# A four-layer hybrid model: two first mixers set later among the filling tiles, sums into x and evacuations of q and k put ahead on their engines

## The chip, the cores and the metric

The kernel runs on one core of one Trainium2 chip. The metric is the device time of one execution in microseconds. The core's engines work in parallel, each through its own queue: TensorE (PE; its weight loads are listed as PEld), VectorE (DVE), ScalarE (ACT), GpSimd (POOL) and SyncE (SP), which here only issues transfers.

## What is computed

1040 tokens (16 meta tokens and 1024 of the sequence) with 1024 features go through four layers, each a normalisation, a projection in, a mixer and a projection out that is added to x:

```python
for i in range(DEPTH):                       # 4
    kind, j = i % N_MIXERS, i // N_MIXERS    # 3 kinds
    u = rmsnorm(h, norm_gain[i])
    if kind == 0:
        y = attention_branch(u, ...)   # 16 heads of q, 4 of k and v, window 128, rope, sinks
    elif kind == 1:
        y = mlstm_branch(u, ...)       # 8 heads, causal conv on q and k, blocks of 128
    else:
        y = hgrn2_branch(u, ...)       # 8 heads, decay per feature
    h = h + jnp.where(valid[None, :, None], y, 0.0)
```

In the second kind (`mlstm`) q and k pass a convolution over four tokens and a SiLU; two gates per head give rows of cumulated decays; then, block by block, a product of k and q weighted by these rows, and a state C carried from block to block. In the third kind (`hgrn2`) the product of q and k is formed level by level with decays in between. In the first kind q and k are normalised per head and rotated (rope) before windowed attention.

## The kernel before, in words

x lies in SBUF for the whole run, features on partitions, in eight tiles `x[:, m, :]`. All work on tokens goes in three chunks of 400, 384 and 256 columns (`CHUNKS`), or in nine blocks (`blk`: one of 16 tokens, eight of 128). To keep fp32 accuracy every factor of a large product is split into a high and a low part (`split`, L193 on ScalarE and L194 on VectorE: `uh`, `ul` from the normalised x, `wh`, `wl` from the weights, `yh`, `yl` from a mixer's result), and three matmuls are made for each product.

**The order on TensorE is written by hand.** The program is a list of steps `[cost, function, pre]`; the cost is in ns of matmul columns at 2.4 per ns (`MM`). `weave(a, b)` merges two lists in proportion to their costs; `later`, `spread` and `chain` put steps at a given distance. A step `[c, lambda: None, None]` does nothing and only takes up c in these sums. At the end the list is run through once. A step's `pre` (load a matrix of weights in two halves into `wr` on SyncE's queue, L205, and split it) is written out as soon as the costs of the steps up to it come to less than `LOOKAHEAD` = 12000.

**The order on the other engines** is not the written one: among the instructions whose inputs and buffers are free, the program's scheduler prefers the one that was written first. Inside `with tc.high_priority(offset=PRIO)` (`PRIO` = 40) an instruction ranks as if written 40 instructions earlier. Steps of the mixers and the splits of `yh`, `yl` are wrapped in it already (`hi`).

Buffers: eight PSUM banks for everything (`psum`, tags pj for projections, pm, po, pt, pa for the mixers and the statistics), six temporaries (`TMPS`), three pairs of split weights, two raw halves (`RAWS`).

**Where the change lies:**

- `proj_out` (L290 to L333): for each chunk and each of eight output tiles m, six matmuls (L321) and then the sum into x on VectorE (L324), which frees the bank. At a layer's last products `fin` follows, which squares the new x for the next norm (L351) and adds the squares up (L355).
- `qk_proj` of `layer_a`: `evac` copies a finished chunk of q or k out of PSUM twice on ScalarE, scaled (L491) and squared (L492), and issues four transfers that rotate the partitions (L495). 2000 later in the list, TensorE sums the squares over the head (L506), from which ScalarE makes the reciprocal root (L337, L338); VectorE applies rope (L511 to L514). In the mixer of this layer, a score step (matmuls L597 and L598, minimum L604, exponential L607, reciprocal L609, product on GpSimd L610) is followed two steps later by a transpose on TensorE (L622).
- `layer_b`, the second layer: `head` is v of head 0 with the gates, `body` begins with q and k of head 0 (`conv_proj`: copy L825, four steps of convolution L828 and L831, SiLU L399 to L403, product L835 or L837). `gate_rows` (L776 to L794) makes the decay rows on eight partitions and writes them to DRAM. Then for each head h its mixer is woven with q, k and v of head h + 1. A mixer begins with a step of no cost that reads two decay rows back, spread over all partitions (`rb` L856, `wb` L857); each block has steps `s1` (product of k and q, L864, transpose of k, L866), `s2` (L885, L887), `s3` (L899, state C at L904) and `s4` (L913).
- `layer_c`, the third layer: for each head, `main` holds five regions of eight levels (X, made at L1111 to L1114 on VectorE and ScalarE) with their matmuls (`levels_mm`: L1127, L1137), `tails` what follows. `weave(main[r], last)` joins each region with the tail of the one before, and the whole is woven with `fill`: what is left of q of head 0, and f and q of head 1.

Of the kernel before, what the change touches and what calls it, by code (L numbers as in the profile page):

```python
# [11 lines left out]
AF = mybir.ActivationFunctionType  # L12
ALU = mybir.AluOpType
# [23 lines left out]
PRIO = 40  # L37
ROWS, TMPS, RAWS, YS = 8, 6, 2, 3
XS = 14
GAP, BURST = 200.0, 1300.0  # L40
GATE_LAG, GATE_COLS = 2000.0, 17000.0
KT_LAG, ATT_LAG = 900.0, 600.0
NORM_AT = (4000.0, 0.7), (5000.0, 0.5), (8000.0, 0.5)
Y_LAST, Y_EARLY, Y_AHEAD = 3, 8, 2500.0
# [66 lines left out]
def hybrid_kernel(ctx: ExitStack, tc: tile.TileContext, ins, out, layers=(0, 1, 2, 3)):  # L111
    nc = tc.nc
    v, s, g, pe, sp = nc.vector, nc.scalar, nc.gpsimd, nc.tensor, nc.sync
# [11 lines left out]
    def nm(x):  # L125
        ctr[0] += 1
        return f"{x}{ctr[0]}"
# [19 lines left out]
    def psj():  # L147
        return psum("pj", 3)
# [15 lines left out]
    x = cpool.tile([P, KT, T], F32, name="x")  # L164
# [27 lines left out]
    def split(src, h, l):  # L192
        s.copy(h, src)  # L193
        v.tensor_tensor(l, src, h.bitcast(F32), op=ALU.subtract)  # L194
# [90 lines left out]
    def hi(fn):  # L285
        def f():
            with tc.high_priority(offset=PRIO):
                fn()

        return f  # L290

    def proj_out(src0, src1, y, chunks=CHUNKS, fin=None, inrow=False):
        st = {}

        def pre0():
            st[0] = weights(src0, "o", inrow=inrow)

        def pre1():
            st[1] = weights(src1, "o", inrow=inrow)

        groups = []
        for n, (c0, cn) in enumerate(chunks):
            grp = []

            def ysplit(k, n=n, c0=c0, cn=cn):
                def fn():
                    yh, yl = (tpool.tile([P, 400], F32R, tag=z, name=nm(z), bufs=YS)[:, :cn] for z in ("yh", "yl"))
                    split(y(k)[:, c0 : c0 + cn], yh, yl)
                    st["y", n, k] = yh, yl

                return [0.0, hi(fn), None]

            def product(m, k, n=n, c0=c0, cn=cn):
                h, l = st[m // 4]
                mc = slice((m % 4) * P, (m % 4 + 1) * P)
                if k == 0:
                    st["p", n, m] = psj()
                acc = st["p", n, m]
                yh, yl = st["y", n, k]
                for i, (a, b) in enumerate(((h, yh), (h, yl), (l, yh))):  # L320
                    pe.matmul(acc[:, :cn], a[:, k, mc], b,  # L321
                              start=(k == 0 and i == 0), stop=(k == 1 and i == 2))
                if k == 1:
                    v.tensor_tensor(x[:, m, c0 : c0 + cn], x[:, m, c0 : c0 + cn], acc[:, :cn], op=ALU.add)  # L324
                    if fin:
                        fin(m, n, c0, cn)

            order = [(m, k) for m in range(KT - Y_LAST) for k in range(2)]
            order += [(m, k) for k in range(2) for m in range(KT - Y_LAST, KT)]
            for m, k in order:  # L330
                pre = (pre0, pre1)[m // 4] if (n == 0 and m % 4 == 0 and k == 0) else None
                grp.append([3 * cn * MM, lambda m=m, k=k, product=product: product(m, k), pre])
            groups.append(([ysplit(0), ysplit(1)], grp))  # L333
        return groups
# [80 lines left out]
    def layer_a(i, j, first, last, fin):  # L415
        win, wout = ins["a_win"][j], ins["a_wout"][j]
        chunks = LAST_CHUNKS if last else CHUNKS
        R = {}
# [66 lines left out]
        def qk_proj(src, gcol, work, fsplit, ch):  # L485
            late = {}

            def evac(acc, n, c0, cn):
                dst, sq, rot = work(n, c0, cn)
                late[n] = dst, sq, rot  # L490
                s.activation(dst, acc[:, :cn], AF.Identity, scale=R["cons"][:, gcol : gcol + 1])  # L491
                s.activation(sq, acc[:, :cn], AF.Square)  # L492
                for q in range(4):
                    o = q ^ 1
                    sp.dma_start(rot[32 * q : 32 * q + 32], dst[32 * o : 32 * o + 32])  # L495

            def finish(n, c0, cn):
                def stat():
                    dst, sq, rot = late[n]
                    b0, bn = CHUNKS[n]  # L500
                    if R.get("cs", (None,))[0] != n:
                        R["cs"] = n, R["mix"].tile([P, 2, 400], F32, tag="cs", name=nm("cs"), bufs=1)
                        sp.dma_start(R["cs"][1][:, :, :bn], ins["rope"][:, :, b0 : b0 + bn].rearrange("a p t -> p a t"))
                    late[n] = dst, sq, rot, R["cs"][1][:, :, c0 - b0 : c0 - b0 + cn]
                    st = psa()
                    pe.matmul(st[:, :cn], R["masks"][:, 0:P], sq, start=True, stop=True)  # L506
                    rstd_from(st, sq, cn, 64)

                def rope():
                    dst, sq, rot, cos_sin = late[n]  # L510
                    v.tensor_tensor(dst, dst, cos_sin[:, 0, :cn], op=ALU.mult)  # L511
                    v.tensor_tensor(rot, rot, cos_sin[:, 1, :cn], op=ALU.mult)
                    v.tensor_tensor(dst, dst, rot, op=ALU.add)
                    v.tensor_tensor(dst, dst, sq, op=ALU.mult)  # L514

                return [(D_Q[0], [4 * cn * MM, stat, None]), (D_Q[1], [0.0, rope, None]),
                        (D_Q[2], fsplit(lambda: late[n][0], n, c0, cn))]

            return proj(src, evac, ch), [finish(n, *c) for n, c in enumerate(ch)]
# [212 lines left out]
    def layer_b(i, j, fin):  # L732
        win, wout = ins["b_win"][j], ins["b_wout"][j]
        R = {}
# [257 lines left out]
        for h in range(8):  # L992
            mx = mixer(h)
            mx, rest = mx[:-3], mx[-3:]
            if h < 7:
                body += weave(mx, flat(qg[h + 1]) + flat(kg[h + 1]) + flat(vg[h + 1]))
                if h < 6:
                    body += weave(rest, gates(h)[:6]) + gates(h)[6:] + flat(zg[h][1]) + flat(outs(oc[h]))
                else:
                    held = rest  # L1000
            else:
                body += weave(held + mx, gates(6) + flat(zg[6][1]))
# [3 lines left out]
    def layer_c(i, j, fin):  # L1006
        win, wout = ins["c_win"][j], ins["c_wout"][j]
        R = {}
# [261 lines left out]
        for h in range(8):  # L1270
            fill = qg[0][2] if h == 0 else []
            if h in (4, 6):
                fill += flat(outs(oc[h - 3]))
            if h < 7:
                fill += flat(fg[h + 1]) + flat(qg[h + 1])
            if h in (1, 3, 5):
                fill += flat(vg[h // 2 + 1])
            for z in {2: (0, 1), 4: (2,), 5: (3,), 7: (4, 5, 6)}.get(h, ()):
                fill += flat(zg[z])
            main, tails, end = mixer(h)  # L1280
            if h:
                tails[0].append(held)
            held = end
            mx = []
            for r in range(5):
                mx += weave(main[r], last)
                last = [[TAIL_LAG, lambda: None, None]] + tails[r]
            body += weave(mx, fill)
# [190 lines left out]
```

## Time and profile before

| | before |
|---|---|
| median of 3 runs | 2635.76 us (2635.3 to 2638.44) |
| the profiled execution | 2632.63 us, its span 2630.8 us |
| granted TensorE clock, mean | 0.995 |
| DVE, ACT, POOL busy | 75%, 64%, 9% of the span |

The first layer runs up to about 490 us of the span, the second to about 1576, the third to about 2178, the fourth to the end. In lines of the timeline, the first number is the start in us, the second the length in us, and what stands in brackets is the idle time of the engine just before and what ended it. "L506 <- ACT t L492" in a list of waits reads: line 506 waited for the instruction of line 492 on ScalarE that writes a tile t. In a table of stretches the busy times of the engines come in the order PE, PEld, DVE, ACT, POOL, each with its count of instructions, and then the granted clock (1.00 is full).

### The profile page before, as it was taken

What the parts mean: (1) busy time and instruction counts of PE and PEld (TensorE: products, weight loads), DVE (VectorE), ACT (ScalarE), POOL (GpSimd) and SP (SyncE); (2) the same over time, 40 slices, a digit from 0 to 9 for tenths busy, and PEclk for the clock granted to TensorE, in tenths of its full rate; (3) what the DMA queues carried; (4) which work ended last, traced back from release to release, by engine and by line L of the source; (5) the groups of instructions that cost most, each with busy time, mean ns of one, the idle gap of its engine ahead of it and who ended that gap; (6) DMA issues with size and microseconds to landing.
All of it is one profiled execution on the core that took longest, in us unless ns stands there. A gap on an engine that the chain in (4) does not pass through costs nothing.

```text
span 2630.8 us, 53986 instructions
## 1 busy us (share of the span) xinstructions
PE 2562.9 (97%) x20246; PEld 2468.6 (94%) x20246; DVE 1976.8 (75%) x5344; ACT 1693.7 (64%) x4374; POOL 249.5 (9%) x502
## 2 busy tenths in 40 slices
PE   7999999989999999999999999999999999999999
PEld 5899989989999999999999999999999998999999
DVE  7887798784747474757475688988888989887896
ACT  7777767565454545454545757878675857867772
POOL 2221231000000000000000000101000000321330
PEclk9999999999999999999999999999999999999999
DMA  4213111011111111111111101111110113212112
GB/s 129 69 49 91 47 44 48 22 63 52 41 57 41 57 41 57 41 53 45 53 45 49 53 30 42 34 34 34 38 38 30 38 50 92 63 39 83 55 37 80
DMA packets 82581, 135.89 MB, mean 52 GB/s; under 512 B 12032, under 2 KB 35712, under 8 KB 82320
## 3 DMA queue, kind: packets, MB, share of 16 engines
q1 hardware_dynamic: 82320, 132.45, 15.9%
q8 instruction: 159, 2.61, 0.4%
q14 instruction: 102, 0.84, 0.1%
HBM read 117.56 MB, written 4.26 MB: 46 GB/s over the span
## 4 chain that ended last, share of the span: by engine, by line
PE 74%; DVE 12%; ACT 8%; DMA 3%; issue 2%; SPq 1%; POOL 1%; DVEq 0%; ACTq 0%; POOLq 0%
PE pj L227 35%; PE pj L321 15%; PE pj L276 10%; ACT Sm L607 1%; PE po L641 1%; PE po L885 1%; PE pt L622 1%; PE pa L899 1%; PE po L887 1%; DVE Sm L604 1%; DVE wl L194 1%; DMA cs<-in_rope 1%; PE pj L272 1%; DVE Pl L625 1%; PE pm L1137 1%
## 5 line engine op out<-in xcount | busy, mean ns | idle before, releaser
L227 PE MATMUL pj<-uh,wh 128*128 128x256 f32 (+2 forms) x2688 | 919.7, 342 | 9.4 <-ACT uh L193 9.4
L227 PE MATMUL pj<-ul,wh 128*128 128x256 f32 (+2 forms) x2688 | 867.2, 323 | 2.7 <-DVE ul L194 2.4
L227 PE MATMUL pj<-uh,wl 128*128 128x256 f32 (+2 forms) x2688 | 863.8, 321 | 0.0
L227 PEld LDWEIGHTS pj<-uh,wh 128*128 128x128 f32 x2688 | 509.3, 189 | 28.6 <-ACT uh L193 13.1
L227 PEld LDWEIGHTS pj<-ul,wh 128*128 128x128 f32 x2688 | 509.5, 190 | 13.8 <-DVE ul L194 6.4
L227 PEld LDWEIGHTS pj<-uh,wl 128*128 128x128 f32 x2688 | 509.0, 189 | 0.1
L193 ACT CAST wh<-wr 128x512 fp32r<-128x512 f32 (+1 forms) x338 | 202.9, 613 | 102.0 <-PE pj L321 31.3
L194 DVE TENSOR_TENSOR wl<-wr,wh 128x512 fp32r<-128x512 f32 (+1 forms) x338 | 232.1, 697 | 48.5 <-ACT wh L193 45.0
L321 PE MATMUL pj<-yh,wh 128*128 128x384 f32 (+2 forms) x768 | 253.1, 330 | 9.9 <-DVE x L324 6.4
L324 DVE TENSOR_TENSOR x<-x,pj 128x384 f32<-128x384 f32 (+2 forms) x480 | 234.6, 509 | 34.1 <-PE pj L321 32.7
L321 PE MATMUL pj<-yl,wh 128*128 128x384 f32 (+2 forms) x768 | 245.3, 319 | 0.3 <-DVE yl L194 0.3
L321 PE MATMUL pj<-yh,wl 128*128 128x384 f32 (+2 forms) x768 | 245.2, 319 | 0.0
L276 PE MATMUL pj<-wh,uh 128*128 128x256 f32 (+1 forms) x768 | 231.9, 302 | 0.0
L276 PE MATMUL pj<-wl,uh 128*128 128x256 f32 (+1 forms) x768 | 216.5, 282 | 0.0
L276 PE MATMUL pj<-wh,ul 128*128 128x256 f32 (+1 forms) x768 | 216.2, 281 | 0.0
L607 ACT ACTIVATE Sm<-Sm,s 128x257 f32<-128x257 f32 (+2 forms) x272 | 130.7, 482 | 91.7 <-DVE s L604 90.3
L610 POOL TENSOR_TENSOR Sm<-Sm,s 128x512 f32<-128x512 f32 (+2 forms) x136 | 141.2, 1038 | 467.1 <-DVE s L609 454.3
L403 ACT ACTIVATE t<-t 128x384 f32<-128x384 f32 (+2 forms) x240 | 117.8, 491 | 88.0 <-DVE t L402 86.4
L402 DVE SCALAR_TENSOR_TENSOR t<-pj,t 128x384 f32<-128x384 f32 (+2 forms) x192 | 98.8, 515 | 81.7 <-ACT t L401 80.0
L321 PEld LDWEIGHTS pj<-yh,wh 128*128 128x128 f32 x768 | 144.2, 188 | 14.7 <-DVE x L324 8.6
L193 ACT CAST yh<-r 128x384 fp32r<-128x384 f32 (+2 forms) x120 | 57.1, 478 | 146.2 <-PE pj L321 132.5
L276 PEld LDWEIGHTS pj<-wh,uh 128*128 128x128 f32 x768 | 144.6, 188 | 2.1
(251 smaller groups left out, 5445.7 us busy)
## 6 DMA issues: line engine op xcount, KB each, us to landing
wr<-in_b_win SPq DMA_DIRECT2D x124, 256.0 KB, 2.8
wr<-in_a_win SPq DMA_DIRECT2D x80, 256.0 KB, 2.9
wr<-in_c_win SPq DMA_DIRECT2D x64, 256.0 KB, 2.8
wr<-in_a_wout SPq DMA_DIRECT2D x32, 256.0 KB, 2.8
wr<-in_b_wout SPq DMA_DIRECT2D x32, 256.0 KB, 2.7
t<-t SPq DMA_DIRECT2D x104, 48.0 KB, 2.0
cs<-in_rope SPq DMA_DIRECT2D x11, 400.0 KB, 3.7
cs<-in_rope SPq DMA_DIRECT2D x11, 384.0 KB, 3.2
```

The costliest lines, as they stand in the source:

```text
L193: s.copy(h, src)
L194: v.tensor_tensor(l, src, h.bitcast(F32), op=ALU.subtract)
L227: pe.matmul(acc[:, :cn], a[:, k, :], b[:, k, c0 : c0 + cn], start=(k == 0 and i == 0), stop=(k == KT - 1 and i == 2))
L272: pe.matmul(acc[:48, :nc], um[0][:, k, :], m[:, kk, :], start=(k == 0 and m is wh), stop=(k == KT - 1 and m is wl))
L276: pe.matmul(acc[:cn, :nc], a[:, k, c0 : c0 + cn], m[:, kk, :], start=(k == 0 and j == 0), stop=(k == KT - 1 and j == 2))
L321: pe.matmul(acc[:, :cn], a[:, k, mc], b, start=(k == 0 and i == 0), stop=(k == 1 and i == 2))
L324: v.tensor_tensor(x[:, m, c0 : c0 + cn], x[:, m, c0 : c0 + cn], acc[:, :cn], op=ALU.add)
L402: v.scalar_tensor_tensor(a[:, :cn], z, 0.0, a[:, :cn], op0=ALU.min, op1=ALU.subtract)
L403: s.activation(a[:, :cn], a[:, :cn], AF.Exp)
L604: v.tensor_tensor_reduce(Sm[:nq, u, :nk], S[:nq, u, :nk], R["masks"][:nq, P + mo : P + mo + nk], -1.0, sinks[u], ALU.add, ALU.min, st[:nq, ...
L607: s.activation(Sm[:nq, u, : nk + 1], Sm[:nq, u, : nk + 1], AF.Exp, scale=-1.0, bias=st[:nq, u : u + 1], accum_out=den[:nq, u : u + 1])
L610: g.tensor_tensor(Sm[:nq, :, :nk], Sm[:nq, :, :nk], den[:nq].rearrange("p (u c) -> p u c", c=1).to_broadcast([nq, 2, nk]), op=ALU.mult)
```

## The change

Four edits. In the second layer, a step of cost 8000 that does nothing is put ahead of the mixer of head 0, before it is woven with q, k and v of head 1. In the third layer, the same with 2500 ahead of the first region of head 0. The sums into x in `proj_out`, and the two copies out of PSUM in `evac` of q and k, get the rank of an instruction written 40 earlier. No arithmetic, buffer or transfer is added or removed.

```diff
-GATE_LAG, GATE_COLS = 2000.0, 17000.0
+GATE_LAG, GATE_COLS, MIX_AHEAD, START_LAG = 2000.0, 17000.0, 8000.0, 2500.0
...
                 if k == 1:
-                    v.tensor_tensor(x[:, m, c0 : c0 + cn], x[:, m, c0 : c0 + cn], acc[:, :cn], op=ALU.add)
+                    with tc.high_priority(offset=PRIO):
+                        v.tensor_tensor(x[:, m, c0 : c0 + cn], x[:, m, c0 : c0 + cn], acc[:, :cn], op=ALU.add)
                     if fin:
                         fin(m, n, c0, cn)
...
             def evac(acc, n, c0, cn):
                 dst, sq, rot = work(n, c0, cn)
                 late[n] = dst, sq, rot
-                s.activation(dst, acc[:, :cn], AF.Identity, scale=R["cons"][:, gcol : gcol + 1])
-                s.activation(sq, acc[:, :cn], AF.Square)
+                with tc.high_priority(offset=PRIO):
+                    s.activation(dst, acc[:, :cn], AF.Identity, scale=R["cons"][:, gcol : gcol + 1])
+                    s.activation(sq, acc[:, :cn], AF.Square)
                 for q in range(4):
...
         for h in range(8):
             mx = mixer(h)
             mx, rest = mx[:-3], mx[-3:]
+            if h == 0:
+                mx.insert(0, [MIX_AHEAD, lambda: None, None])
             if h < 7:
                 body += weave(mx, flat(qg[h + 1]) + flat(kg[h + 1]) + flat(vg[h + 1]))
...
             held = end
-            mx = []
+            mx = [] if h else [[START_LAG, lambda: None, None]]
             for r in range(5):
                 mx += weave(main[r], last)
```

## The prediction, made before the changed kernel was run

> **What bounds the kernel now.** I read the page's first block, then the waits of PE, then the timeline around each long one.
>
> ```profile
> span 2630.8 us, 53986 instructions
> PE 2562.9 (97%) x20246; PEld 2468.6 (94%) x20246; DVE 1976.8 (75%) x5344; ACT 1693.7 (64%) x4374; POOL 249.5 (9%) x502
> ```
>
> PE sets the end: 2562.9 of 2630.8 us. Whatever this change does can only come out of the 67.9 us in which PE does nothing, or out of a slow clock behind such a pause, because it removes no matmul.
>
> ```profile
> PE pa L506 <- ACT t L492: 9.3, 7, 2.2
> PE pm L864 <- DVE r L837: 8.9, 1, 8.9
> PE pt L622 <- POOL Sm L610: 6.5, 7, 2.1
> PE pj L321 <- DVE x L324: 6.4, 6, 1.4
> ...
> PE pm L1137 <- DVE X L1114: 2.1, 1, 2.1
> PE pm L597 <- DVE x L324: 1.8, 1, 1.8
> ```
>
> Columns: total us, times, longest. Of the pauses, four kinds touch the edited lines: L864 is the first mixer matmul of the second layer, L1137 lies in the first mixer of the third, L324 is the sum into x, L492 the second evacuation of q or k. Together 8.9 + 2.1 + 6.4 + 1.8 + 9.3 = 28.5 us. L622 belongs to the attention chain, which the edit touches only through the order on ACT and DVE.
>
> What a pause costs afterwards is seen in the granted clock (columns: stretch, length, busy us of PE, PEld, DVE, ACT, POOL, clock, DMA share, GB/s):
>
> ```profile
> 545.80:554.70 8.90, 0.01 (x1) 0.02 (x2) 8.55 (x23) 6.07 (x15) 0.00 (x0) 0.67 0.25 91
> 554.70:559.10 4.40, 4.40 (x17) 4.33 (x18) 3.44 (x10) 2.94 (x8) 0.00 (x0) 0.50 0.18 60
> 559.10:565.00 5.90, 5.90 (x30) 4.62 (x29) 3.43 (x12) 2.66 (x8) 0.10 (x1) 1.00 0.01 3
> ...
> 1651.00:1654.80 3.80, 3.80 (x43) 3.74 (x36) 3.55 (x14) 2.50 (x9) 0.00 (x0) 0.55 0.02 4
> ...
> 2385.40:2388.80 3.40, 3.38 (x10) 3.18 (x11) 3.27 (x7) 3.26 (x9) 1.14 (x1) 0.52 0.25 87
> ```
>
> After the 8.9 us pause PE works 4.40 us at half clock: 2.2 us lost. After the pause of L1137, 3.80 us at 0.55 lose 1.7; after the longest pause of L506, 3.40 us at 0.52 lose 1.6. So the ceiling is 28.5 + 5.5 = 34.0 us.
>
> **The second layer's lead (8000 ns ahead of the mixer of head 0).** PE's order is written by hand, so the lead moves PE's instructions for certain.
>
> ```profile
> 545.49 0.28 PE L227 MATMUL pj<-uh,wl 128*128 128x256 f32 x1
> 554.68 0.23 PE L864 MATMUL pm<-q,r 128*16 128x16 f32 x2 [8.92 <-DVE r L837]
> ```
>
> ```profile
> 531.64 2.31 DVE L780 TENSOR_TENSOR_SCAN r<-r,r 8x1040 f32<-8x1040 f32 x1
> 533.88 2.68 DVE L783 TENSOR_TENSOR_SCAN r<-ones,r 8x16 f32<-8x16 f32 x9
> 554.07 0.57 DVE L837 SCALAR_TENSOR_TENSOR r<-r,t 128x400 f32<-128x400 f32 x1
> ```
>
> PE has finished q and k of head 0 at 545.8 and waits for the first columns of k, whose convolution ends on DVE at 554.6: DVE was late with it after the gate rows (two of whose steps are shown, 5.0 us). By the code's own costs the mixer of head 0 (without its last three steps) is 14,650 and its filling tiles 42,987. With the lead, 8000 of 22,650 = 35.3% of the filling goes first: 15,183, so 17 steps of 960 to 1000 (640 for the short chunk): all of q of head 1 and five steps of its k, 15.4 us. The mixer's first matmul then comes no sooner than 545.8 + 15.4 = 561.2, and its k is ready at 554.6: 6.6 us to spare. Saved: 8.9 + 2.2 = 11.1.
>
> What is late next? Those 17 steps hand DVE more convolutions while it is still behind.
>
> ```profile
> 560.00:600.00 40.00, 40.00 (x268) 38.40 (x268) 29.57 (x89) 23.53 (x63) 0.49 (x5) 1.00 0.10 31
> ```
>
> ```profile
> 600.00:610.00 10.00, 10.00 (x82) 9.81 (x81) 2.05 (x9) 2.83 (x8) 0.10 (x1) 1.00 0.10 38
> ```
>
> From 545.8 to 600 DVE does 8.55 + 3.44 + 29.57, about 42 us (0.9 us lie between the rows); PE will be there 11.1 us sooner, after 43.1 us. DVE would have to be 98% busy, if its work stayed where it is. It doesn't: the lead moves four fifths of the mixer's DVE work behind k of head 1, where now, at 600 to 610, DVE is busy 2.05 of 10 us. The waiting convolutions keep their PSUM banks meanwhile.
>
> ```profile
> 546.68 0.47 ACT L825 COPY t<-pj 128x400 f32<-128x400 f32 x1
> ...
> 556.29 0.34 ACT L825 COPY t<-pj 128x256 f32<-128x256 f32 x1
> ```
>
> The three chunks of k of head 0 were all done on PE at 545.8 and left PSUM from 546.7 to 556.6: three of eight banks are tied up by such a backlog, five are left for one running product and the four kinds of mixer banks. I take 1.0 us for what this adds: 10.1 saved. Bounds: 11.1 if nothing new appears, 0 if the whole pause moves to another wait.
>
> Moved with the mixer are its two broadcast reads on SP (rb, wb), and the lead counts as 8000 of the 12,000 by which weights are announced, so q's weights of head 1 are announced some 4 us ahead instead of 12. Both matter only if the queues follow the written order closely.
>
> ```profile
> 520.02 1.29 DVE L194 TENSOR_TENSOR wl<-wr,wh 128x512 fp32r<-128x512 f32 x2 [7.34 <-ACT wh L193]
> 524.20 0.69 DVE L194 TENSOR_TENSOR wl<-wr,wh 128x512 fp32r<-128x512 f32 x1 [2.89 <-ACT wh L193]
> 525.08 0.69 DVE L194 TENSOR_TENSOR wl<-wr,wh 128x512 fp32r<-128x512 f32 x1 [0.18 <-ACT wh L193]
> ...
> 528.67 0.68 DVE L194 TENSOR_TENSOR wl<-wr,wh 128x512 fp32r<-128x512 f32 x1
> ...
> 531.04 0.67 DVE L194 TENSOR_TENSOR wl<-wr,wh 128x512 fp32r<-128x512 f32 x1
> ```
>
> There are three weight buffers: the splits at 520 are q's of head 0, those at 524 and 525 its k's, those at 528.7 and 531.0 q's of head 1, ready 14 us before PE is free for them: more than 12 ahead, so they run when a buffer is free, not when they are announced. I cost this at nothing; if the cover goes, they queue behind DVE's backlog up to 554.6, and 554.6 - 545.8 = 8.8 us of the saving is gone.
>
> [...] The row: a 2.1 us pause before 1651 is followed by clock 0.55. [...]
>
> **The third layer's lead (2500 ns).** By the same arithmetic the first mixer has 27,159 against 23,360 of filling. The pause isn't at its beginning:
>
> ```profile
> 1650.84 0.33 PE L1137 MATMUL pm<-X 128*32 128x32 f32 x16 [2.10 <-DVE X L1114]
> ```
>
> It is its fourth region, some 17,100 into the mixer (1260 + 2900 + 2900 of the regions before it, 2848 + 3595 of the tails woven into those, some 3600 of its own levels and the tail beside them). Ahead of that stand 17,100/27,159 = 62.9% of the filling now, 19,600/29,659 = 66.0% then: 0.7 us more. DVE is busy all through (3.55 of 3.80 us in the row from 1651), so the work, not the start, is late. I take 0.8 saved; bounds 3.8 (pause and clock gone) and minus 2.1 (such a pause once more, from a denser mixer).
>
> **Sums into x ahead (L324).** All 20 output products are touched; the seven pauses total 6.4 + 1.8 = 8.2 us. One of them:
>
> ```profile
> 2175.56 1.29 DVE L194 TENSOR_TENSOR wl<-wr,wh 128x512 fp32r<-128x512 f32 x2 [0.24 <-ACT wh L193]
> 2176.77 0.55 DVE L355 TENSOR_TENSOR t<-t,t 128x384 f32<-128x384 f32 x1
> 2177.24 0.55 DVE L324 TENSOR_TENSOR x<-x,pj 128x384 f32<-128x384 f32 x1
> ```
>
> The sum frees the bank PE waits for. It gets the rank of an instruction written 40 earlier, some six products' matmuls: the norm's squares (L355) fall behind it, weight splits announced 12 us ahead don't. I take two thirds, 5.5. Bounds 8.2 and 0; a loss would be the norm's, and is in the last term.
>
> **Evacuations of q and k ahead (L491, L492).** The seven pauses total 9.3 us, 10.9 with the clock.
>
> ```profile
> 2382.60 0.62 ACT L193 CAST wh<-wr 128x512 fp32r<-128x512 f32 x1
> 2383.12 0.48 ACT L491 ACTIVATE t<-pj,cons 128x256 f32<-128x256 f32 x1
> ...
> 2385.00 0.36 ACT L492 ACTIVATE t<-pj 128x256 f32<-128x256 f32 x1
> ```
>
> ```profile
> 256.08 0.70 PE L506 MATMUL pa<-t,masks 128*128 128x256 f32 x2 [1.82 <-ACT t L492]
> ```
>
> ```profile
> 254.56 0.47 ACT L491 ACTIVATE t<-pj,cons 128x256 f32<-128x256 f32 x1 [1.03 <-DVE t L513]
> 255.64 0.38 ACT L492 ACTIVATE t<-pj 128x256 f32<-128x256 f32 x1 [0.61 <-DVE t L514]
> ```
>
> At 2383 ACT was busy with other work, which a higher rank can pass. At 255 it was idle, waiting for DVE to release a buffer: rank can't help there, and that pause (1.8 us, up to 256.1) stays. Of the other 9.1 I take 5.0; bounds 9.1 and 0. The four DMAs behind each evacuation go out with it, so SP is held less, not more.
>
> **New waits.** What goes ahead puts something back: attention's exponentials, unit splits, squares. Nearest row: L622, 6.5 us in seven pauses. I take half as much again, 3.0; bounds 0 and 31 (the rival below).
>
> **Sum:** 10.1 + 0.8 + 5.5 + 5.0 - 3.0 = 18.4 us, against the profiled execution's own 2632.63 (span 2630.8 and 1.8 around it): 2614.2. The median is 3.1 above that execution: **2617.4**.
>
> **Rivals.** *Leads alone*: the priorities give and take the same; 10.9 us, 2624.9. For it: waits in the attention layers are many and short. Against: rows like 2176.77, where a square stands ahead of the sum.
>
> *The wait moves*: the second layer's pause comes back as a wait for weights or banks, 8.8 of 11.1 lost, and 10.1 becomes 2.3: 2625.2. For it: the 98%. Against: the free DVE from 600. With "leads alone" as well it would be 2632.7, no change; that is also what a change that misses its aims would look like.
>
> *Slower*: the evacuations, at the attention chain's own rank, delay it on ACT.
>
> ```profile
> L491 ACT ACTIVATE t<-pj,cons x54: 452/566/605, 27.3 to 2482.9; 128x384 f32<-128x384 f32 x26, 128x256 f32<-128x256 f32 x18, 128x400 f32<-128x400 f32 x10
> L492 ACT ACTIVATE t<-pj x54: 361/483/509, 27.7 to 2484.0; 128x384 f32<-128x384 f32 x26, 128x256 f32<-128x256 f32 x18, 128x400 f32<-128x400 f32 x10
> ```
>
> A pair takes 0.566 + 0.483 = 1.05 us, and with the six into rows there are 60. If half of them push an exponential back when its transpose has no slack, that is 31 us: 2617.4 + 31 = 2648. It makes the kernel slower by over 0.2% from 23 of 60 on ((18.4 + 5.3) / 1.05). Against: PE waits for that chain only seven times now.
>
> **How the numbers follow.** 0.2% is 5.3 us, about what a measurement of this kernel can tell from no change. Forecast 0.60 (its own range 2606 to 2624), leads alone 0.15, the wait moves 0.08, both or a miss 0.07, slower 0.10. Faster 0.60 + 0.15 + 0.08 = 0.83, same 0.07, slower 0.10. The low end takes every upper bound, 11.1 + 3.8 + 8.2 + 9.1 = 32.2 us: 2603.5, so 2604; the high end is 2630, which leaves out the last two cases, 0.17.
>
> **What would show it.** Right: no wait of L864 for L837, clock 1.00 from 540 to 600 in the second layer; fewer and shorter waits of L321 for L324 and of L506 for L492, that at 256 still there; the third layer's pause near 1640 little changed. Wrong: PE waits for wl or for L825 near 546 to 575 (the wait moved); L622's total well above 6.5 or L363's waits for L355 at the layers' ends (the priorities took as much as they gave).

## The result, and the profile after

| | before | after |
|---|---|---|
| median | 2635.47 us (12 runs) | 2639.16 us (12 runs) |
| ratio, 95% interval | | 1.0014 [1.0005, 1.0023] |
| span of the profiled execution | 2630.8 us | 2633.3 us |

No faster: 2639.16 lies 3.7 us above before and 9 us above the upper end of the predicted range. The page's first block of the changed kernel, then its waits of PE (total us, times, longest):

```profile
span 2633.3 us, 53915 instructions
PE 2564.4 (97%) x20246; PEld 2468.9 (94%) x20246; DVE 1979.8 (75%) x5344; ACT 1692.1 (64%) x4374; POOL 250.6 (10%) x502
```

```profile
PE pa L364 <- DVE t L356: 14.7, 5, 5.0
PE pa L508 <- ACT t L494: 12.4, 9, 3.2
...
PE pt L624 <- POOL Sm L612: 8.7, 16, 1.2
...
PE pm L1141 <- DVE X L1118: 2.1, 3, 0.9
...
PE pj L321 <- DVE x L325: 1.1, 2, 0.7
...
PE po L887 <- DVE W L874: 0.9, 1, 0.9
...
PE pm L599 <- DVE x L325: 0.4, 1, 0.4
```

Lines below the edits are one to four numbers higher than before. The sum into x is now L325, the add of squares L356, the statistics of the norm L364; the evacuations are L493 and L494, the head sum L508.

Two aims are met: the 8.9 us pause of L864 is gone, and the waits for the sum into x fell from 8.2 us (6.4 + 1.8) to 1.5. Two things rose: the statistics' wait for the adds of squares, now 14.7 us in five pauses, and the head sums' wait for the evacuations, from 9.3 to 12.4 us, the very wait that the evacuations' rank was to shorten. Before has that row with two pauses only, at the program's start:

```profile
PE pa L363 <- DVE t L355: 5.5, 2, 4.9
```

The other three are new, one at the end of each of the first three layers. The timeline of PE, after:

```profile
259.08 1.22 PE L508 MATMUL pa<-t,masks 128*128 128x256 f32 x2 [3.19 <-ACT t L494]
...
500.12 0.97 PE L364 MATMUL pa<-t,ones 128*128 128x384 f32 x2 [3.55 <-DVE t L356]
...
1580.30 1.65 PE L364 MATMUL pa<-t,ones 128*128 128x384 f32 x2 [2.92 <-DVE t L356]
...
2185.34 0.91 PE L364 MATMUL pa<-t,ones 128*128 128x384 f32 x2 [2.88 <-DVE t L356]
```

The second layer's beginning in stretches (columns as in the prediction):

```profile
545.20:559.00 13.80, 13.80 (x98) 13.54 (x97) 12.65 (x29) 8.14 (x23) 0.00 (x0) 1.00 0.35 121
559.00:570.00 11.00, 11.00 (x72) 11.00 (x71) 9.81 (x25) 7.30 (x18) 0.00 (x0) 1.00 0.15 49
570.00:580.00 10.00, 9.13 (x56) 7.54 (x55) 9.30 (x24) 6.55 (x18) 0.10 (x1) 1.00 0.17 52
```

PE is busy throughout at full clock, but for one pause of 0.87 us at 575.88. DVE is busy 31.76 of 34.80 us, 91%: the full engine that I feared is there, and it doesn't stop PE.

To place gains and losses I compare when PE begins its n-th matmul in two kernels (worked out from the traces; the number of matmuls is the same). Each row is how late the kernel is against before, in us, at the matmul that before begins at the time on top; minus is ahead:

```
                 260     480     500     545     640    1560    1600    2175    2200    2215    2629
after           4.32    5.65    9.61    9.61   -0.03    1.08    5.47    4.65    6.09    4.90    2.49
leads           0.18    0.62    0.63    0.63   -7.71   -7.60   -7.56   -7.14   -7.14   -7.15   -6.83
leads_ev        5.45    6.48    6.46    6.47   -3.33   -3.15   -3.12   -3.95   -3.95   -3.31    0.05
leads_x         2.46    2.94    6.85    6.85   -1.50   -1.45    1.71    1.62    4.91    3.73    2.82
leads_xmid      2.43    2.93    3.30    3.30   -5.06   -4.86   -4.83   -4.97   -4.95   -4.99   -6.39
leads_x_add     2.29    3.01    5.49    5.49   -4.28   -3.94   -1.26   -0.78    1.36    1.37    1.24
leads_x_sq     -0.35    0.48    5.80    5.80   -4.18   -4.17   -0.04   -0.65    6.21    4.45    4.50
leads_ev_xmid   5.34    6.68    7.02    7.03   -2.66   -1.64   -1.59   -2.42   -2.40   -0.23   -1.57
start_only      1.19    1.30    1.29    1.29    1.26    1.26    1.26    1.12    1.12    1.11    1.41
leads_12        1.20    1.50    1.51    1.51   -8.44   -8.01   -7.98   -7.65   -7.63   -7.71   -6.91
leads_ev_wh     6.52    6.75    6.76    6.77   -3.01   -2.87   -2.83   -3.00   -1.11   -1.02   -0.61
leads_ev_rope   0.22    1.31    1.31    1.31   -8.47   -8.30   -8.26   -8.23   -8.22   -2.40   -3.41
leads_ev_two    0.27    0.96    0.95    0.96   -8.72   -8.62   -8.58   -8.94   -8.66   -8.64   -8.55
```

The first row tells the story of the change: 5.65 us lost in the first layer, 4.0 more at its end, 9.6 won by the second layer's lead (9.61 to -0.03), 4.4 lost at that layer's end, 1.4 at the third's, 3.6 won back in the last layer. The other rows are the experiments.

Each row is one execution, and that sets how finely it can be read. VectorE and ScalarE do the same instructions in the same order in before, start_only, leads and leads_12 through the whole first layer, and yet these four stand up to 1.5 us apart at 480. leads_x and leads_x_sq, in the same order up to 486 us, stand 2.5 us apart there: in leads_x two stretches of half clock came (at 128 us, where the clock is 0.57 over 4.00 us, last section, and at 258 us), about 1.7 us each, and in leads_x_sq none. So a step of one or two us in a single row shows little; steps of 3 us and more that several rows repeat, and the medians of several runs, carry the argument.

### The profile page after: what moved, and what is told of

Read it like the earlier page. It is cut to its first block, busy times and chain, and to the rows that moved or that the text cites. A ratio compares the mean times of both kernels' runs of the same rounds, so it can differ in the third digit from the quotient of the medians.

```text
span 2633.3 us, 53915 instructions
## 1 busy us (share of the span) xinstructions
PE 2564.4 (97%) x20246; PEld 2468.9 (94%) x20246; DVE 1979.8 (75%) x5344; ACT 1692.1 (64%) x4374; POOL 250.6 (10%) x502
## 4 chain that ended last, share of the span: by engine, by line
PE 74%; DVE 12%; ACT 8%; DMA 2%; issue 2%; SPq 1%; POOL 0%; DVEq 0%; ACTq 0%; POOLq 0%
PE pj L227 35%; PE pj L321 14%; PE pj L276 10%; ACT Sm L609 1%; PE po L887 1%; PE po L643 1%; PE pt L624 1%; PE pa L901 1%; DVE Sm L606 1%; DVE wl L194 1%; PE po L889 1%; DVE x L325 1%; PE pj L272 1%; PE pm L1141 1%; DVE qs L464 1%
## 5 line engine op out<-in xcount | busy, mean ns | idle before, releaser
L227 PEld LDWEIGHTS pj<-uh,wh 128*128 128x128 f32 x2688 | 509.1, 189 | 28.0 <-ACT uh L193 12.4
L325 DVE TENSOR_TENSOR x<-x,pj 128x384 f32<-128x384 f32 (+2 forms) x480 | 236.2, 509 | 36.7 <-PE pj L321 34.5
L321 PEld LDWEIGHTS pj<-yl,wh 128*128 128x128 f32 x768 | 144.7, 188 | 2.9 <-DVE yl L194 2.5
```

The lines of the kernel that those rows point to most:

```text
L227: pe.matmul(acc[:, :cn], a[:, k, :], b[:, k, c0 : c0 + cn], start=(k == 0 and i == 0), stop=(k == KT - 1 and i == 2))
L321: pe.matmul(acc[:, :cn], a[:, k, mc], b, start=(k == 0 and i == 0), stop=(k == 1 and i == 2))
```

## The experiments

No kernel here leaves out any of the work. "Leads" are the first two edits. Medians stand beside the kernel's ratio to before on the same chip; between the chips the median of before itself goes from 2634.6 to 2636.4 us, so a difference of one or two us between medians of different groups shows nothing.

**The parts alone.** The leads without any rank; with the evacuations' rank; with the sums' rank; with both, the sums' rank left out at a layer's last products.

> Only the two leads, no higher ranks. Theory A (the leads give what was forecast, the ranks take it back, most of it at the ends of the layers): the second layer's pause and its slow clock go (9.6 us net), the third layer gives 0.6, PE waits for the norm's squares (L355 before, three waits of 2.9 to 3.6 us in the changed kernel) are not there: 10 us below the kernel before, ratio 0.996. Rival B (the lead only shifts the pause, PE gets back behind later): ratio 0.999 to 1.001, with new pauses of some 8 us between 560 and 700 us.

> The leads and the higher rank of the evacuations of q and k, sums into x as before. Theory A: about 8 us below the kernel before (10.2 of the leads; the first layer loses some 5.7 and the last wins 3.6 by the evacuations), ratio 0.997; no waits of 3 us for the squares at the layers' ends. Rival C (the loss at the layers' ends comes from the changed order as a whole, not from the sums): those waits are there here too, ratio 1.000 to 1.002.

> The leads and the higher rank of the sums into x, evacuations as before. Theory A: the three waits for the squares are there and take some 11 us with the clock behind them, which is what the leads gave: ratio 1.000 (2633 to 2638). Rival D (the evacuations are what takes the gain): ratio 0.994 to 0.996.

> As the changed kernel, but the last sums of a layer, those that the next norm follows, keep their old rank; the sums inside the layers keep the higher one. Theory A: the 11 us at the layers' ends come back: 2628, ratio 0.997. Rival E (the sums inside the layers, which delay the attention chain, are what costs): as the changed kernel, 1.001.

The last one's edit, against the changed kernel:

```diff
-                    with tc.high_priority(offset=PRIO):
-                        v.tensor_tensor(x[:, m, c0 : c0 + cn], x[:, m, c0 : c0 + cn], acc[:, :cn], op=ALU.add)
+                    if fin:
+                        v.tensor_tensor(x[:, m, c0 : c0 + cn], x[:, m, c0 : c0 + cn], acc[:, :cn], op=ALU.add)
+                    else:
+                        with tc.high_priority(offset=PRIO):
+                            v.tensor_tensor(x[:, m, c0 : c0 + cn], x[:, m, c0 : c0 + cn], acc[:, :cn], op=ALU.add)
```

| | median us | ratio [95%] |
|---|---|---|
| leads | 2625.46 | 0.9965 [0.9953, 0.9978] |
| leads_ev | 2633.65 | 0.9995 [0.9986, 1.0004] |
| leads_x | 2633.65 | 0.9996 [0.9987, 1.0004] |
| leads_ev_xmid | 2631.18 | 0.9990 [0.9981, 0.9999] |

The leads alone give 9.2 us (2635 x 0.0035, interval 5.8 to 12.4). Either rank on top of them costs 8.2 us (2633.65 - 2625.46), the evacuations' more than I had expected; the two together cost 13.7 (2639.16 - 2625.46), less than their sum. In the table of delays the sums lose at the ends of layers (leads_x: 3.9 from 480 to 500, 3.2 from 1560 to 1600, 3.3 from 2175 to 2200), where leads loses nothing; the evacuations lose in the first layer (5.45 by 260, leads 0.18) and in the last (4.0 from 2200 on, leads 0.3). What leads_x loses by 260 is no loss of the sums: it is the two stretches of half clock that leads_x_sq doesn't have. leads_ev_xmid, the changed kernel without the ranks at the ends, gives back 8.0 us of the changed kernel's time where I had expected 11, and loses nothing at the second layer's end (-1.64 to -1.59) or the third's (-2.42 to -2.40): there theory A holds. What it still lacks against leads is the evacuations' part.

**Doses, and the ends left out.** The third layer's lead alone; the second layer's with 12000; leads with the sums' rank inside layers only; the changed kernel with `fin` (squares and adds for the next norm) at the higher rank too.

> Only the lead of 2500 in the third layer. Theory A: 0.5 to 1.5 us below the kernel before (the pause of 2.1 us comes back as four of 0.6 to 0.9, the slow clock behind it goes), ratio 0.9995. Rival: 0.998, the size at which the third layer would have given what the second did.

> Both leads, the second layer's 12000 instead of 8000. Theory A (what is left of the second layer's pause, 0.7 us at 567 and 3.4 us of half clock behind it, comes from VectorE still being behind with the convolutions): a later mixer meets a freer VectorE, the pause goes, 2 us below the run with leads of 8000, ratio 0.9957. Rival F (the denser mixer is what pauses): more pauses between 560 and 610, ratio 0.997 to 0.998.

> The leads, and the higher rank only for sums into x inside the layers, evacuations as before. Theory A: no waits for squares at the layers' ends; 2625 to 2627, as with the leads alone, ratio 0.996 to 0.997; what the sums win inside the last layer (2 us) they lose inside the first. Rival E: the sums inside the layers cost 4 us or more, ratio 0.998 or above.

> The changed kernel, with the squares of the new x and their sums at the same higher rank as the sums into x. Theory A: with the order between sum and square as it was before, the three waits for the squares at the layers' ends (9.4 us and slow clock) go or fall below 1 us each: 2630 or less, ratio 0.998. Rival G (it is the normalised tiles and weight splits of the next layer that fill VectorE there, whatever the squares' rank): the waits stay, 2638, ratio 1.001.

| | median us | ratio [95%] |
|---|---|---|
| start_only | 2634.19 | 0.9996 [0.9987, 1.0005] |
| leads_12 | 2624.69 | 0.9958 [0.9945, 0.9970] |
| leads_xmid | 2625.19 | 0.9959 [0.9945, 0.9973] |
| all_fin | 2638.48 | 1.0009 [1.0000, 1.0017] |

The third layer's lead alone can't be told from no change, and its row gains nothing where it acts (1.26 to 1.12 from 1600 to 2175). Against its theory, the longer lead of the second layer didn't remove the pause that is left there: 0.82 us at 571.58 stay. Only the half clock behind the pause (0.50 over 3.40 us in leads, last section) doesn't come this time, which is the 1.6 us by which its row wins more than that of leads (1.51 to -8.44, against 0.63 to -7.71); the medians, 2624.69 and 2625.46, are too near to be told apart.

Without the ends, the sums' rank costs nothing and gives nothing: 2625.19 against 2625.46. The waits for the adds are back to the two at the start in leads_xmid:

```profile
PE pa L367 <- DVE t L359: 5.5, 2, 4.9
```

With `fin` raised as well, the three waits at the ends fell to 2.23, 1.92 and 1.65 us, and the time did not follow: the 2630 expected if squares and adds were all that the sums push back didn't come.

**The ends of layers: the cast, the squares or the adds?** First I suspected ScalarE's order. In leads_x the squares stand behind a cast of the next layer's weights that waits for PE to free the buffer, so I moved this cast to GpSimd:

```diff
-            split(raw, h[:, z], l[:, z])
+            if kind == "g":
+                g.tensor_copy(h[:, z], raw)
+                v.tensor_tensor(l[:, z], raw, h[:, z].bitcast(F32), op=ALU.subtract)
+            else:
+                split(raw, h[:, z], l[:, z])
```

> Both leads, all sums into x ahead, and the high parts of the second layer's first matrices (v of head 0 with the gates, 816 and 272 columns) cast on GpSimd instead of ScalarE; nothing else moved. Theory E (at the end of the first layer the squares of the new x stand on ScalarE behind a cast of these weights that waits 2.56 us for TensorE to free its buffer, so the statistics of the next norm come late): the squares no longer stop near 488 to 491, the wait of L364 for L356 near 497 falls from 3.55 us to under 1, and the delay that the end of the first layer adds (480 to 500 us of the span) falls from 3.9 us to under 1.5; the ends of the second and third layers keep their 3 us each, so the time is some 3 us under leads with sums, 2630 to 2631.5. Rival J (the statistics are late through VectorE's order, which does the sums and the units ahead of the adds): the wait near 497 stays at 3 us or more and the time at 2633 to 2634.

2635.83 us, 1.0005 [0.9996, 1.0013]: the theory fell. The wait near 497 grew. PE and then ScalarE of this kernel (its sum into x is L329, its squares L356, its statistics L368):

```profile
496.48 1.28 PE L368 MATMUL pa<-t,ones 128*128 128x384 f32 x2 [4.61 <-DVE t L360]
```

```profile
489.24 0.42 ACT L356 ACTIVATE v<-x 128x256 f32<-128x256 f32 x1 [2.84 <-DVE x L329]
489.57 0.92 ACT L356 ACTIVATE t<-x 128x384 f32<-128x384 f32 x2
```

With the cast gone, a square of the next chunk (256 columns) stands in its place and waits 2.84 us for its sum, with the squares that the statistics need behind it. So that cast alone was not what held them up. Two kernels then raised only the adds (the diff, against leads_x) or, in the same way, only the squares:

```diff
-                (v if self.row is None or n == 0 else g).tensor_tensor(self.acc[n], self.acc[n], q, op=ALU.add)
+                with tc.high_priority(offset=PRIO) if self.row is None else ExitStack():
+                    (v if self.row is None or n == 0 else g).tensor_tensor(self.acc[n], self.acc[n], q, op=ALU.add)
```

> Both leads, all sums into x ahead, and the adds of the squares for the next norm (L356, VectorE) at the same higher rank, the squares (L352, ScalarE) at their old one. Theory J (the sums push the adds back on VectorE, and the adds release the temporaries that the next squares need): the waits of L364 for L356 at the three ends fall from about 3 us each to under 1, and the time from 2633.7 to 2625 to 2628. Theory E (the squares are late on ScalarE's queue behind an instruction that waits): the waits stay at 2.5 us or more and the time at 2632 to 2635.

> Both leads, all sums into x ahead, and the squares for the next norm (L352, ScalarE) at the same higher rank, the adds (L356, VectorE) at their old one. Theory E: the waits of L364 for L356 fall to under 1 us each, 2625 to 2628. Theory J: they stay at 2.5 us or more, and the time stays at 2632 to 2635.

Adds: 2632.05 us, 0.9986 [0.9977, 0.9995]. Squares: 2638.94 us, 1.0016 [1.0007, 1.0025]. The same wait in leads_x, with the adds up, and with the squares up, from the three lists of waits:

```profile
PE pa L364 <- DVE t L356: 14.9, 5, 4.9
```

```profile
PE pa L365 <- DVE t L357: 12.1, 5, 4.9
```

```profile
PE pa L365 <- DVE t L357: 17.3, 5, 4.9
```

Raising the adds takes away a third of the waits at the three ends, where the theory asked for two thirds and more (1.95, 2.41 and 2.03 us remain of 3.55, 2.91 and 2.88), and the time misses the 2625 to 2628 that it gave; raising the squares makes it worse (4.07, 4.17 and 3.44). So it isn't the squares' rank; the adds' place on VectorE is part of the cause, not all of it. The stretch before the first layer's end, in before and after:

```profile
484.00:496.00 12.00, 10.86 (x84) 10.27 (x83) 11.67 (x29) 8.42 (x21) 0.89 (x11) 1.00 0.20 64
```

```profile
488.00:500.20 12.20, 8.65 (x66) 8.44 (x64) 11.88 (x28) 7.02 (x18) 1.16 (x11) 1.00 0.13 33
```

VectorE is full in both, 97% (11.67 of 12.00; 11.88 of 12.20). Rank makes no time there; it only says which of its jobs is late. After, its timeline shows which (one add per feature tile must be done before the statistics at 500.12):

```profile
493.02 0.55 DVE L356 TENSOR_TENSOR t<-t,t 128x384 f32<-128x384 f32 x1
493.49 0.41 DVE L325 TENSOR_TENSOR x<-x,pj 128x256 f32<-128x256 f32 x1
493.82 0.63 DVE L386 SCALAR_TENSOR_TENSOR t<-x,ngain,t 128x400 f32<-128x400 f32 x1
494.36 1.07 DVE L194 TENSOR_TENSOR wl<-wr,wh 128x408 fp32r<-128x408 f32 x2
495.50 0.58 DVE L194 TENSOR_TENSOR ul<-t,uh 128x400 fp32r<-128x400 f32 x1
496.00 0.41 DVE L325 TENSOR_TENSOR x<-x,pj 128x256 f32<-128x256 f32 x1
496.33 0.55 DVE L356 TENSOR_TENSOR t<-t,t 128x384 f32<-128x384 f32 x1
```

Between two adds lie sums of the next chunk, a unit of the next layer, a split of weights: 3.3 us from one add to the next, while PE runs out of work. To what the 2 us are owed that remain at each end with the adds up stays open; that the sums at the ends cause them is shown (leads_xmid).

**The evacuations: the casts, or the temporaries?** ScalarE of leads, with two casts of weights and the evacuation of a 400-column chunk, and the same three of leads_ev, where that evacuation is ahead in rank and comes later:

```profile
240.15 0.61 ACT L193 CAST wh<-wr 128x512 fp32r<-128x512 f32 x1
...
242.68 0.61 ACT L193 CAST wh<-wr 128x512 fp32r<-128x512 f32 x1
...
244.77 0.58 ACT L491 ACTIVATE t<-pj,cons 128x400 f32<-128x400 f32 x1
```

```profile
245.42 0.62 ACT L193 CAST wh<-wr 128x512 fp32r<-128x512 f32 x1 [0.54 <-DMA wr<-in_a_win]
247.53 0.62 ACT L193 CAST wh<-wr 128x512 fp32r<-128x512 f32 x1 [1.50 <-DMA wr<-in_a_win]
248.06 0.59 ACT L492 ACTIVATE t<-pj,cons 128x400 f32<-128x400 f32 x1
```

It stands behind casts that wait for their transfers. The two casts before these came at 238.91 and 239.42 instead of 234.51 and 236.91, so the two raw halves came free later. The loads into them went out at 242.68 and 243.88 instead of 236.42 and 239.85, the first right behind four rotations that hold SP from 239.92 to 242.56. I put weights back in front, in the two attention layers (`up` is `PRIO` for their q, k, v and gates):

```diff
             raw = wpool.tile([P, 512], F32, tag="raw", name=nm("wr"), bufs=RAWS)[:, : width // 2]
-            sp.dma_start(raw, src[:, z])
-            split(raw, h[:, z], l[:, z])
+            with tc.high_priority(offset=up) if up else ExitStack():
+                sp.dma_start(raw, src[:, z])
+                split(raw, h[:, z], l[:, z])
```

> Both leads, the evacuations of q and k ahead, and in the two attention layers also the loads and the splits of the weights (L193, L194, L205) at the same higher rank. Theory D (the evacuations cost because ScalarE's queue is in order: what they pass are the casts of the weights, these come some 3 to 4 us later, the raw halves are released later, and the next evacuation then stands behind a cast that waits for its transfer): with the casts back in front, the delay at the end of the first layer falls from 6.5 us (leads with evacuations) to under 2, the longest wait of the head sums (L508) for L494 from 3.2 to about 2, and the time comes to 2626 to 2629 against 2625.5 for the leads alone and 2633.7 for leads with evacuations. Rival H (what is passed are attention's exponentials and the copies of yh and uh, the weights don't matter): the delay at the end of the first layer stays at 5 to 7 us, the product's waits (L611 to L623) stay at 7 us or more, and the time stays at 2631 to 2635.

2631.32 us, 0.9988 [0.9979, 0.9996]. Half right: from 2215 on it adds 0.4 us (leads_ev 3.4), after 1.9 at the third layer's end. But at the end of the first layer it is as late as leads_ev, 6.75 us: 3.4 of these come between 235 and 262 us, as in leads_ev (3.4), and 2.8 in the first 100 us. The latter can't be laid on the weights, for leads_ev_two (below), which doesn't raise them in this layer, loses 2.4 in the same 100 us. ScalarE near 245:

```profile
243.58 0.47 ACT L493 ACTIVATE t<-pj,cons 128x256 f32<-128x256 f32 x1 [0.18 <-DVE t L515]
244.88 0.38 ACT L494 ACTIVATE t<-pj 128x256 f32<-128x256 f32 x1 [0.83 <-DVE t L516]
...
248.55 0.60 ACT L493 ACTIVATE t<-pj,cons 128x400 f32<-128x400 f32 x1 [0.43 <-DVE t L515]
249.44 0.51 ACT L494 ACTIVATE t<-pj 128x400 f32<-128x400 f32 x1 [0.29 <-DVE t L516]
```

Now evacuations wait for rope (L515, L516) of an earlier chunk. A chunk in the making holds three of the six temporaries, so the evacuation of a third cannot begin before the rope of the first releases one. The next kernel raises root and rope as well:

```diff
+                    with tc.high_priority(offset=PRIO):
+                        rstd_from(st, sq, cn, 64)
...
+                    with tc.high_priority(offset=PRIO):
+                        v.tensor_tensor(dst, dst, cos_sin[:, 0, :cn], op=ALU.mult)
...
```

> Both leads, the evacuations of q and k ahead, and also the steps that follow on the same chunk: the reciprocal root (L338, L339, ScalarE) and the four rope operations (VectorE) at the same higher rank. Theory M (six temporaries hold two chunks; an evacuation put ahead of its rope waits in ScalarE's queue for a temporary, and all behind it wait too): with the rope as far ahead, the delay that 235 to 262 us of the span adds falls from 3.3 us to under 1, the longest wait of the head sums from 3.2 to about 2, and the time from 2633.7 to 2627 to 2630. Rival N (rank has nothing to do with it; the chunk's rotations and the one rope table on SP's queue set the pace): 235 to 262 still adds 3 us or more and the time stays at 2631 to 2636.

2629.04 us, 0.9978 [0.9969, 0.9987]: theory M holds in the first layer. The head sums' pause near 256 falls from 3.22 us in leads_ev to 0.29, and the first layer's loss is gone (1.31 at 480, as much as in start_only). This also says what the late casts do there. The second of the two casts shown above comes at 249.44, later still than in leads_ev, but the evacuation of 400 columns, now at 246.72, stands ahead of it: in the first layer it isn't the late casts that cost, but what stands behind them. The last layer now loses 5.8 us between 2200 and 2215 instead, and the longest wait of the head sums, 2.79 us, lies there (2399). PE, and VectorE just before:

```profile
2197.33 0.58 PE L227 MATMUL pj<-uh,wh 128*128 128x256 f32 x1 [3.92 <-ACT uh L193]
```

```profile
2194.38 0.56 DVE L445 TENSOR_TENSOR r<-r,r 64x400 fp32r<-64x400 f32 x1
2194.87 0.47 DVE L385 SCALAR_TENSOR_TENSOR t<-x,ngain,v 128x256 f32<-128x256 f32 x1
```

The units of the norm (L385), from which `uh` comes, stand behind rope and the splits of k. Then each remedy in the layer where it helped, rope in the first and weights in the last:

> Both leads, the evacuations of q and k ahead, root and rope ahead in the first layer only, the loads and splits of the weights ahead in the last layer only. Theory D and M together (what the evacuations cost is the late temporaries in the first layer and the late casts in the last, 8.2 us with all): the delay at 480 us is about 1.3 us, the last layer from 2215 to the end adds under 1 us, and the time is 2625 to 2628, as good as the leads alone (2625.5) and 6 to 8 us under leads with evacuations (2633.7). Rival N (the two gains don't add, for the waits move to whatever was passed, the splits of uh above all): 2629 to 2632.

2625.57 us, 0.9960 [0.9946, 0.9974]: 8.1 of the 8.2 us are back, and no more. So the evacuations' cost sits in the rope of the first layer and the weights of the last, where putting these ahead as well takes it away, and the ranks together give nothing over the leads alone (2625.46). Rope and weights ahead without the evacuations wasn't run, so it stays open whether these two alone would gain something that the evacuations then take.

**A faster version.** Second layer's lead 12000, sums ahead inside layers only, evacuations as before; and the same with the third layer's lead at 6000.

> Second layer's lead of 12000 instead of 8000, third layer's of 2500, the sums into x ahead except at the last products of a layer; the evacuations at their old rank. The two parts measured singly: leads with 12000 2624.7, leads of 8000 with these sums 2625.2, leads alone 2625.5. Theory A (each part is small and they touch different places): 2623.5 to 2625. Rival K (both only move the same waits): 2624.5 to 2626, no better than either; both expect it clearly faster than before and than the changed kernel, by 10 us or more.

> As leads_12_xmid, with the third layer's lead at 6000 instead of 2500. Theory F (the third layer's first pauses come from its work being dense on VectorE and ScalarE, and a later start only moves them): the waits of L1138 and its neighbours between 1640 and 1655 keep their sum of some 2.8 us, the time stays within 1 us of leads_12_xmid. Rival L (the mixer begins too early): the pauses near 1640 to 1655 vanish and the time falls by 2 to 3 us.

2624.27 us, 0.9962 [0.9948, 0.9975], and 2625.74, 0.9968 [0.9955, 0.9980]. The first is 14.9 us under the changed kernel (13.7 by the ratios), but it can't be told from leads_12 or leads. More lead in the third layer gives nothing: that kernel is 1.5 us slower, a little more than theory F allowed, its pauses from 1640 to 1660 sum to 3.9 us against 2.7, and one of them is now 1.66 us long.

## Why the prediction was wrong

**The second layer's lead: right.** 10.1 us predicted, 9.6 measured in the changed kernel (9.61 to -0.03), 8.3 in leads (0.63 to -7.71). The residual that I put at 1.0 is a pause of 0.73 to 0.87 us; in leads a stretch of half clock follows it (0.50 over 3.40 us, last section), which is most of the difference between 9.6 and 8.3. No wait for weights or banks took its place.

**The third layer's lead: small, as said.** 0.8 predicted. The list of waits holds the same 2.1 us as before, now in three pauses of at most 0.9. From 1600 to 2175 leads goes from -7.56 to -7.14 and start_only from 1.26 to 1.12: nothing gained that a row can show. A lead of 6000 gained nothing either, so the work is late, not the start.

**Sums into x: wrong in sign.** The step read: the norm's squares fall behind the sum, "I take two thirds, 5.5", with the loss left to a common last term. The waits did fall, by 6.7 us (8.2 to 1.5), but the rank cost 8.2 us. A sum frees one of eight banks; an add stands at the head of a chain (statistics, root, units, splits) on which the next layer's first product hangs. I had counted the first and not asked what the second is worth, though VectorE's row (11.67 of 12.00) could have been read in the profile of before. Inside the layers, where no such chain hangs on it, the rank neither gave nor cost (leads_xmid), so of the 5.5 us forecast nothing came.

**Evacuations: wrong in sign.** "A higher rank can pass" other work on ScalarE, 5.0 us; "SP is held less, not more". They cost 8.2. What they passed were casts, and with the casts went the raw halves and the next transfers; putting the weights back in front undid the loss in the last layer. And the limit that I had seen for one pause (254.56, waiting for VectorE to release a buffer) is that of the whole chain in the first layer, where only rope put ahead as well undid the loss. The pause that I said would stay at 1.8 us grew to 3.19.

**New waits: 3.0 us, with the two terms at their value, for what came to 24.** This term failed. The ranks were to give 10.5 us and gave -13.7 (2625.46 - 2639.16): 24.2 us apart. I took the nearest row, L622, and half as much again. It rose by only 2.2 us, 6.5 to 8.7. The loss sat in two other places, of which I named one beforehand as what would show me wrong: the statistics' waits at the layers' ends. The slower rival named one of the two edits that cost, and the wrong victim: attention's chain wasn't what paid, for in leads_xmid the same wait stands at 9.5 us (leads 6.8) and the time is that of leads. That the forecast of the leads held is no luck, for the pause went as described and nothing took its place; that the sum came out 21.8 us off (2639.2 against 2617.4) is the two ranks, 7.5 forecast (10.5 - 3.0) and -13.7 measured.

Theory D takes ScalarE's queue to be in order. That it always is wasn't shown; what was seen are instructions that begin only behind one that waits, though the product or the sum that they read was done. The evacuation at 248.06 (leads_ev) stands behind a cast that waits 1.50 us, though PE had ended its product by 245.93; the one at 247.00 in the changed kernel stands behind a cast that waits 1.52 us, its product ended by 244.67; the square at 489.57 (leads_x_gcast) stands behind one that waits 2.84 us, though its own sum had ended at 484.83.

## What to carry to other kernels

On an engine that was full in a stretch, as VectorE was here (97%), a rank gave no time, it chose who waited: before raising an instruction, find what it will pass and how much of the critical engine's work hangs on that. A pause in a list of waits is not a price for shortening it, since a raised instruction can wait for its own buffer (2.34 us at 257.56 in the changed kernel, for rope) or behind another that waits (1.50 us before 248.06 in leads_ev). Here, moving independent matmuls into a pause won 9 us, and reordering the engines that caused the pauses lost 14.

## What the runs showed of the hardware

In leads a pause of 0.73 us was followed by half clock some time later. Its PE, and the stretches after the pause:

```profile
566.77 0.59 PE L885 MATMUL po<-v,W 16*16 16x257 f32 x2 [0.73 <-DVE W L872]
```

```profile
568.00:569.20 1.20, 1.20 (x7) 0.61 (x5) 0.84 (x4) 1.20 (x5) 0.00 (x0) 0.99 0.00 0
569.20:572.60 3.40, 3.40 (x17) 3.40 (x17) 3.40 (x13) 2.89 (x11) 0.10 (x1) 0.50 0.00 0
572.60:576.00 3.40, 3.40 (x27) 3.27 (x27) 3.06 (x11) 2.14 (x7) 0.00 (x0) 1.00 0.02 5
```

PE is busy again for 2.4 us before the clock halves, and it is busy all through the 3.40 us at 0.50, which lose 1.7. The same pause of 0.73 us is followed by a stretch of half clock in leads_x and leads_xmid too (from 545 to 640 their rows win 8.35 and 8.36 us, that of leads 8.34), and by full clock in leads_ev (its row wins 9.80); so is the pause of 0.87 us in the changed kernel (1.00 from 576.50 to 600).

Nor did the order of instructions decide at 128 us, where the clock is 0.57 in leads_x and 1.00 in leads_x_sq. In leads_x and leads_x_sq, PE, VectorE and ScalarE do the same up to 128 us in the same order, and shortly before it PE waits 2.11 and 2.14 us for the same product of GpSimd. The next 4 us of the two:

```profile
128.00:132.00 4.00, 4.00 (x21) 4.00 (x20) 3.01 (x9) 3.65 (x12) 1.68 (x2) 0.57 0.07 16
```

```profile
128.00:132.00 4.00, 4.00 (x35) 4.00 (x34) 3.24 (x9) 3.95 (x12) 2.15 (x2) 1.00 0.11 29
```

What decides isn't shown.
